# Squares, sums and transposed keys in the head stage of a hybrid layer: one change to a Trainium2 kernel

## The chip, the cores and the metric

The kernel runs on one core of a Trainium2 chip. The metric is the device time of one execution in microseconds (us), lower is better. Times of the kernel before are 1087.89 to 1088.5, median 1088.14 (3 runs); one more execution was profiled. The engines are called PE (TensorE, with its weight loads as PEld), DVE (VectorE), ACT (ScalarE), POOL (GpSimd) and SP (SyncE, which here only issues transfers). Each engine works through its own instructions in the order in which the program issues them; semaphores tie the engines together.

## What is computed

One layer over 256 positions of width 2048, all float32. Of the reference, this is what matters here:

```python
qa, ka, va, fa, qb, kb, vb = jnp.split(h @ w_in_l, splits, axis=-1)     # h = rms_norm(x)
qa = rms_norm(to_heads(qa, N_HEADS_FOX), q_norm_l)       # 8 heads of 128, normalized head by head
ka = rms_norm(to_heads(ka, N_HEADS_FOX), k_norm_l)
out_a = forgetting_attention(qa, ka, to_heads(va, N_HEADS_FOX), c)      # softmax(q k / sqrt(d) + c_t - c_s) v
out_b = stick_breaking_attention(to_heads(qb, N_HEADS_SB), to_heads(kb, N_HEADS_SB), to_heads(vb, N_HEADS_SB))
merged = jnp.concatenate([rms_norm(from_heads(out_a), out_norm_fox_l),
                          rms_norm(from_heads(out_b), out_norm_sb_l)], axis=-1)
x = x + merged @ w_out_l
x = x + conv_ffn(rms_norm(x), ...)                       # up, causal convolution, gate, down
```

The head norms of qa and ka need, for every position and head, the sum of 128 squares.

## The kernel before

**Products in two parts.** Each weight tile arrives as float32 in `w_raw` (5 buffers, loaded by SP, 1 MB each). ACT casts it to a rounded part `w_hi` (line 277, 3 buffers), DVE subtracts to get the rest `w_lo` (line 285, called "split" below). PE multiplies with both: eight matmuls with `w_hi`, four with `w_lo`, twelve for one product of four row blocks (`in_three`, line 305).

**Units and steps.** The combined projection is done in five units (`unit`, lines 546 to 632): A holds the queries and keys of the first four forgetting heads, B those of the second four, C the first stick-breaking queries and keys, V the stick-breaking values, D the second stick-breaking queries and keys. A unit is 11 steps that form a scheme of seven products with fewer multiplications and four plain ones. Steps 4, 6, 9 and 11 are plain and hold two sets of twelve matmuls, the others one. Weights of a step are loaded six steps ahead (sums of two weight tiles, line 593, four steps ahead, and accumulating transfers on POOL's queue), cast and split two steps ahead. The results of a product are taken out of a PSUM bank by ACT (line 601) or added by DVE (line 607), and a bank is written again by a later step, which waits for that. Among these, DVE's addition out of bank a behind step 7 is issued at step 8, after the cast and split for step 10, and step 9's second set writes bank a again.

**Turns.** Side work is written as Python generators. `tick` (line 246) advances them all by one `yield`; it is called after every step and in the middle of every plain step. This is a "turn": turns 1, 2, 3 belong to steps 1, 2, 3, turns 4 and 5 to step 4, 6 to step 5, 7 and 8 to step 6, 9 to step 7, 10 to step 8, 11 and 12 to step 9, 13 to step 10, 14 and 15 to step 11. The order of all instructions on each engine follows from it, with no reordering later. In a turn the running heads go first, then their products in plain float32 (what stands behind `yield FLOATS`, lined up for all heads that reach it in that turn), then the other tasks. Heads wait in a queue, and one starts at most every third turn (`STAGGER`).

**Rows to heads.** When a unit is finished, its `done` function is one of the other tasks of the next unit. For the forgetting heads it is `fox_rows(half)` (line 693): half 0 runs in the turns of unit B, half 1 in those of unit C. Before, turn by turn: turns 1 to 4 square one of four row tiles each (128 positions by 4 heads of 128; keys first, `order`), with four activations per tile whose accumulator gives the sum of squares of one head. At turn 4 DVE starts the reciprocal root (line 171), at turn 6 ACT takes logarithm and exponential, DVE ends it and multiplies the two key tiles (line 710), at turn 7 the two query tiles.

- Half 0 sends its keys `kA0` through the transposing transfer at turn 7 (`send_heads`): ACT spreads the float32 words into planes of 16 bits (line 646), SP issues two transposing transfers (line 650). The queries are transposed on PE at turn 9 (`to_heads`, line 687) and taken out by ACT at turn 10 (line 691), and behind that the keys' planes are joined again (`take_heads`, line 655, one tile on ACT, one on DVE). Heads 0 to 3 may start from turn 11 on.
- Half 1 transposes the keys `kA1` on PE at turn 8, takes them out at turn 9 and transposes the queries there, takes these out at turn 10. Heads 4 to 7 may start from turn 11 on.

A forgetting head (`fox_head`, line 787) splits its queries and keys (792 on ACT, 793 on DVE), two turns later multiplies them on PE (798 to 804) and has DVE mask and take the maxima (807 to 810), two turns later takes exponentials (816, 817) and DVE scales (819 to 821), and so on to its output at line 860, thirteen turns after its start.

**Stick-breaking heads.** `sb_rows(1)` sends the keys `kB1` through the transfer, transposes the queries on PE one turn later, takes them out at the next, and joins the keys (line 655, both tiles on ACT) at the turn behind that. In `sb_head`, after a head's output, DVE adds the head's squares to a running sum (line 923) behind the output's low part (line 919).

Of the kernel before, what the change touches and what calls it, by code (L numbers as in the profile page):

```python
# [12 lines left out]
AF = mybir.ActivationFunctionType  # L13
ALU = mybir.AluOpType
AX = mybir.AxisListType
# [4 lines left out]
NT = S // P  # L20
KT = D // P
HD = 128
NH = 8
# [24 lines left out]
def hybrid_layer(  # L48
# [20 lines left out]
    act, dve = nc.scalar, nc.vector  # L69
# [43 lines left out]
    gq = const.tile([P, 1], F32, name="gq")  # L113
# [20 lines left out]
    zeros = ccol.rearrange("p a b -> p (a b)")[:, :P]  # L134
# [204 lines left out]
    oFox = late.tile([P, NH, S], F32, name="oFox")  # L339
# [11 lines left out]
    def heads_tile(name):  # L351
        return at.tile([P, 4, S], F32, name=name, tag="qk", bufs=2)
# [25 lines left out]
    tile_of = {}  # L378
# [264 lines left out]
    def send_turned(rows, room, moves=(act.copy, dve.tensor_copy)):  # L643
        planes = room.bitcast(U16).rearrange("p h s -> p (h s)").rearrange("p (t c) -> p t c", t=NT)
        for t, (move, (source, words)) in enumerate(zip(moves, rows)):
            move(
                planes[:, t].rearrange("p (b f) -> p b f", b=2),
                source.bitcast(U16).rearrange("p (f b) -> p b f", b=2),
            )
            nc.sync.dma_start_transpose(  # L650
                words.bitcast(U16).rearrange("p (g s) -> p g s", s=P), planes[:, t]
            )
# [7 lines left out]
    def send_heads(rows, n, key, moves=(act.copy, dve.tensor_copy)):  # L660
        tile_of[key] = heads_tile(key)
        send_turned([(rows[n, t], rows[n, t]) for t in range(NT)], tile_of[key], moves)

    def take_heads(rows, n, key, moves):
        for t, move in enumerate(moves):
            take_turned(move, rows[n, t], t, tile_of[key])
# [13 lines left out]
    def to_heads(rows, which, keys, scales):  # L680
        for n, key, scale in zip(which, keys, scales):
            dst = tile_of[key] = heads_tile(key)
            pss = []
            for t in range(NT):
                ps = psb.tile([P, 4, P], F32, name="ps_h", tag="t")
                for h in range(4):
                    nc.tensor.transpose(ps[:, h, :], rows[n, t][:, h * HD : (h + 1) * HD], ident)
                pss.append(ps)
            yield
            for t in range(NT):  # L690
                act.activation(dst[:, :, t * P : (t + 1) * P], pss[t], AF.Identity, scale=scale)

    def fox_rows(half):
        def done(rows):
            order = [(1, 0), (1, 1), (0, 1), (0, 0)]
            ss = small.tile([P, 4, 4], F32, name="ss", tag="ss")
            rn = small.tile([P, 4, 4], F32, name="rn", tag="rn")
            for m, nt in enumerate(order):
                for h in range(4):
                    act.activation(  # L700
                        zeros, rows[nt][:, h * HD : (h + 1) * HD], AF.Square,
                        accum_out=ss[:, m, h : h + 1],
                    )
                if m < 3:
                    yield
            flat = "p a b -> p (a b)"
            yield from rsqrt(rn.rearrange(flat), ss.rearrange(flat), 1.0 / HD, 16)
            for m, nt in enumerate(order):
                r3 = rows[nt].rearrange("p (h d) -> p h d", h=4)
                dve.tensor_tensor(r3, r3, rn[:, m, :].unsqueeze(2).to_broadcast([P, 4, HD]), op=ALU.mult)  # L710
                if m % 2:
                    yield
                    if m == 1 and not half:
                        send_heads(rows, 1, "kA0", (act.copy, act.copy))
            while started["fox"] < 4 * half:
                yield
            if half:
                yield from to_heads(rows, (1, 0), ("kA1", "qA1"), (1.0, gq))
            else:
                yield  # L720
                yield from to_heads(rows, (0,), ("qA0",), (gq,))
                take_heads(rows, 1, "kA0", (act.copy, dve.tensor_copy))
            for h in range(4 * half, 4 * half + 4):
                waiting.append(fox_head(h, half))

        return done

    def sb_rows(half):
        def done(rows):
            if half:  # L730
                while started["sb"] < 4:
                    yield
                yield
                send_heads(rows, 1, "kB1", (act.copy, act.copy))
                yield
                yield from to_heads(rows, (0,), ("qB1",), (QSCALE,))
                yield
                take_heads(rows, 1, "kB1", (act.copy, act.copy))
            else:
                while started["fox"] < NH:  # L740
                    yield
                yield
                yield
                yield from turned_heads(rows)
            ready.add(f"qB{half}")
            if "vB" in ready:
                start_sb(half)

        return done

    def start_sb(half):
        for h in range(4 * half, 4 * half + 4):
            waiting.append(sb_head(h, half))
# [111 lines left out]
    def sb_head(h, half):  # L865
        q, k = tile_of[f"qB{half}"][:, h % 4, :], tile_of[f"kB{half}"][:, h % 4, :]
        (hi, lo), v1 = tile_of["vB01"], tile_of["vB"][half, 1]
        yield FLOATS
        ps = psb.tile([P, 512], F32, name="ps_z", tag="t")[:, : 3 * P].rearrange("p (a b) -> p a b", a=3)
        z0, z1 = ps[:, 0:2, :].rearrange("p a b -> p (a b)"), ps[:, 2, :]  # L870
        zz = ps.rearrange("p a b -> p (a b)")
        mm = nc.tensor.matmul
        mm(z0, k[:, :P], q, start=True, stop=False)
        mm(z1, k[:, P:], q[:, P:], start=False, stop=True)
        started["sb"] += 1
        diagonal = ps[:, 0::2, :]
        dve.tensor_tensor(diagonal, diagonal, maskB, op=ALU.add)
        yield
        e = tmp.tile([P, 3 * P], F32, name="e", tag="pr")
        act.activation(e, zz, AF.Abs)  # L880
        act.activation(e, e, AF.Exp, scale=-1.0)
        act.activation(e, e, AF.Ln, bias=1.0)
        dve.scalar_tensor_tensor(e, zz, 0.0, e, op0=ALU.max, op1=ALU.add)
        yield
        yield
        sps = tmp.tile([P, 2, 3 * P], F32R, name="sps", tag="sps")
        act.copy(sps[:, 0, :], e)
        dve.tensor_tensor(sps[:, 1, :], e, f32(sps[:, 0, :]), op=ALU.subtract)
        yield
        yield  # L890
        for i in range(2):
            mm(zz, ntri[:, :P], sps[:, i, :], start=False, stop=False, skip_group_check=True)
        for i in range(2):
            mm(ps[:, 1, :], ntri[:, P:], sps[:, i, 2 * P :], start=False, stop=i == 1, skip_group_check=True)
        yield
        w = tmp.tile([P, 3 * P], F32, name="w", tag="pT")
        act.activation(w, zz, AF.Exp)
        if h < NH - 1:
            ws = tmp.tile([P, 2, 3 * P], F32R, name="ws", tag="sps")
            act.copy(ws[:, 0, :S], w[:, :S])  # L900
            dve.tensor_tensor(ws[:, 1, :S], w[:, :S], f32(ws[:, 0, :S]), op=ALU.subtract)
        yield
        po = psb.tile([P, S], F32, name="ps_o", tag="t")
        hs = slice((h % 4) * HD, (h % 4 + 1) * HD)
        h0 = slice(h * HD, (h + 1) * HD)
        if h < NH - 1:
            yield from weighted(po, hi[:, h0], lo[:, h0], v1[:, hs], ws, w[:, S:])
        else:
            yield FLOATS
            mm(po, tile_of["vB"][half, 0][:, hs], w[:, :S], start=True, stop=False)  # L910
            mm(po[:, P:], v1[:, hs], w[:, S:], start=False, stop=True)
        yield
        open_outputs()
        if h >= 2:
            oSb.append(rows_tile(f"oSb{h}", 0 if h >= 4 else 1, F32R).rearrange("p (a s) -> p a s", a=2))
        o = oSb[h]
        act.activation(o[:, 0, :], po, AF.Identity, scale=g_sb[:, h : h + 1])
        sq = squared(po, 1, h)
        dve.scalar_tensor_tensor(
            o[:, 1, :], po, g_sb[:, h : h + 1], f32(o[:, 0, :]), op0=ALU.mult, op1=ALU.subtract  # L920
        )
        if sq is not None:
            dve.tensor_tensor(ssq[1], ssq[1], sq, op=ALU.add)

    unit(0, WF, row_tiles("rA", 0), fox_rows(0))
# [609 lines left out]
```

## Time and profile before

| | us |
|---|---|
| median of 3 runs | 1088.14 |
| profiled execution | 1089.65 |
| span of the profiled execution (first to last instruction) | 1087.9 |
| PE busy | 1082.6 |
| DVE busy | 929.5 |
| ACT busy | 776.1 |
| granted clock of TensorE | 1.0 |

A row of the timeline gives the start and the duration in us, the engine, the line, the operation, what is written and read, how many instructions are merged (x2), and in brackets the idle time of the engine before it with what ended it. Merged rows give the time from the first start to the last end. A duration includes a tail in which the next instruction already runs, so a sum over many instructions goes by their starts. In the list of transfers the last number is the median time from issue to landing.

### The profile page before, as it was taken

The page shows a single profiled execution, that of the slowest core. Times are in us where ns is not written, and L with a number is a line of the kernel's source. Part 1 is how long each engine was busy: PE and PEld are TensorE (multiplying, and loading weights), DVE is VectorE, ACT ScalarE, POOL GpSimd, SP SyncE. Part 2 cuts the span into 40 slices and gives each one's busy share as a digit, 9 for nine tenths or more (in the row PEclk, how much of TensorE's full clock was granted, in tenths as well). Part 3 has the DMA queues.
Part 4 walks back from the last instruction along what each step waited for, and adds up shares of the span by engine and source line. Part 5 has one row for each costly group of instructions (what it writes and reads, how often), then busy time and mean ns, then how long its engine had stood idle before and what let it go on. Part 6 is the DMA issues. An engine that isn't in the chain of part 4 may idle for free.

```text
span 1087.9 us, 14614 instructions
## 1 busy us (share of the span) xinstructions
PE 1082.6 (100%) x5635; PEld 932.2 (86%) x5635; DVE 929.5 (85%) x928; ACT 776.1 (71%) x981; POOL 59.0 (5%) x53
## 2 busy tenths in 40 slices
PE   9999999999999999999999999999999999999998
PEld 9988888888878888888888888888888888888887
DVE  5988899898997877779888988889888898879896
ACT  6767798887876857667766767667767766667663
POOL 0000000001000000000000000000000010000000
PEclk9999999999999999999999999999999999999999
DMA  8897988999876666579899597987969698996995
GB/s 311 267 274 234 306 190 241 245 258 290 244 231 222 193 201 195 192 182 263 252 242 300 172 274 250 255 287 178 310 195 294 219 245 261 232 308 168 284 244 156
DMA packets 192688, 262.85 MB, mean 242 GB/s; under 512 B 22105, under 2 KB 115691, under 8 KB 192619
## 3 DMA queue, kind: packets, MB, share of 16 engines
q1 hardware_dynamic: 169162, 214.59, 59.5%
q0 software_dynamic: 23280, 47.19, 24.5%
q8 instruction: 44, 0.72, 0.3%
q14 instruction: 26, 0.20, 0.1%
q10 hardware_dynamic: 176, 0.14, 0.0%
HBM read 255.48 MB, written 2.10 MB: 237 GB/s over the span
## 4 chain that ended last, share of the span: by engine, by line
PE 89%; DVE 5%; issue 2%; DMA 2%; ACT 1%; DVEq 0%; ACTq 0%; POOLq 0%
PE pu L1268 41%; PE bank_a L305 16%; PE bank_b L305 10%; PE bank_c L305 6%; PE acc_o L305 5%; PE acc_v L425 4%; PE bank_e L305 3%; DVE w_lo L285 2%; DMA w_raw<-in_w_down_dram 2%; PE acc L305 2%; ACT w_hi L277 1%; PE ps_x L195 1%; PE ps_o L775 0%; DVE w_raw L996 0%; DVE xb L1290 0%
## 5 line engine op out<-in xcount | busy, mean ns | idle before, releaser
L285 DVE TENSOR_TENSOR w_lo<-w_raw,w_hi 128x2048 fp32r<-128x2048 f32 (+2 forms) x251 | 555.7, 2218 | 120.5 <-ACT w_hi L277 119.6
L277 ACT CAST w_hi<-w_raw 128x2048 fp32r<-128x2048 f32 (+2 forms) x251 | 464.4, 1853 | 205.1 <-PE pu L1268 84.4
L1268 PE MATMUL pu<-hT,w_hi 128*128 128x512 f32 x1408 | 333.5, 389 | 0.0
L1268 PEld LDWEIGHTS pu<-hT,w_hi 128*128 128x128 f32 x1408 | 262.9, 188 | 53.7
L1268 PEld LDWEIGHTS pu<-hT,w_lo 128*128 128x128 f32 x1408 | 180.0, 191 | 6.6
L1268 PE MATMUL pu<-hT,w_lo 128*128 128x256 f32 x1408 | 182.0, 283 | 0.0
L1321 POOL DMA_DIRECT2D w_raw<-in_w_down_dram x31 | 39.8, 1302 | 714.7 <-DVE w_lo L285 383.1
L1193 ACT ACTIVATE tap<-up,ccol 128x256 f32<-128x256 f32 x176 | 74.6, 495 | 0.0
L305 PE MATMUL bank_a<-w_hi,hT 128*128 128x512 f32 x192 | 48.6, 395 | 0.0
L305 PEld LDWEIGHTS bank_a<-w_hi,hT 128*128 128x128 f32 x192 | 35.2, 188 | 6.9
L305 PE MATMUL bank_b<-w_hi,s 128*128 128x512 f32 x160 | 40.1, 392 | 0.2 <-DVE xb L1290 0.2
L305 PE MATMUL bank_a<-w_hi,s 128*128 128x512 f32 x160 | 40.0, 392 | 0.0
L305 PE MATMUL bank_a<-w_hi,g 128*128 128x512 f32 x152 | 38.0, 392 | 0.0
L425 PE MATMUL acc_v<-w_hi,hT 128*128 128x344 f32 x192 | 36.1, 330 | 0.0
L305 PEld LDWEIGHTS bank_b<-w_hi,s 128*128 128x128 f32 x160 | 28.8, 189 | 5.8 <-issue 0.6
L305 PEld LDWEIGHTS bank_a<-w_hi,s 128*128 128x128 f32 x160 | 28.9, 189 | 5.2
L1186 ACT ACTIVATE gate<-up,ccol 128x256 f32<-128x256 f32 x44 | 24.1, 594 | 11.5 <-DVE up L1179 6.2
L1198 DVE TENSOR_TENSOR gate<-gate,tap 128x512 f32<-128x512 f32 x44 | 30.3, 688 | 2.3
L1198 DVE TENSOR_TENSOR val<-val,tap 128x512 f32<-128x512 f32 x44 | 30.3, 688 | 2.3
L305 PE MATMUL acc_o<-w_hi,oSb 128*128 128x512 f32 x128 | 31.7, 396 | 0.0
L1179 DVE TENSOR_TENSOR up<-t,R 128x512 f32<-128x512 f32 x44 | 30.5, 692 | 1.5
L305 PEld LDWEIGHTS bank_a<-w_hi,g 128*128 128x128 f32 x152 | 27.4, 189 | 5.0
(312 smaller groups left out, 1427.4 us busy)
## 6 DMA issues: line engine op xcount, KB each, us to landing
w_raw<-in_w_up_dram SPq DMA_DIRECT2D x88, 1024.0 KB, 6.8
w_raw<-in_w_down_dram SPq DMA_DIRECT2D x44, 1024.0 KB, 7.1
w_raw<-in_w_in_dram SPq DMA_DIRECT2D x40, 1024.0 KB, 6.8
w_raw<-in_w_down_dram POOLq DMA_DIRECT2D x31, 1024.0 KB, 9.9
w_raw<-in_w_out_dram SPq DMA_DIRECT2D x16, 1024.0 KB, 6.2
w_raw<-in_w_in_dram POOLq DMA_DIRECT2D x10, 1024.0 KB, 9.9
w_raw<-in_w_in_dram SPq DMA_DIRECT2D x13, 516.0 KB, 5.3
xb<-in_x_dram POOLq DMA_DIRECT2D x4, 512.0 KB, 9.3
```

The costliest lines, as they stand in the source:

```text
L195: nc.tensor.transpose(ps[:, j, t * P : (t + 1) * P], x2[:, t, (k + j) * P : (k + j + 1) * P], ident)
L277: copy(hi[:, :n], raw[:, :n])
L285: dve.tensor_tensor(lo[:, :n], raw[:, :n], f32(hi[:, :n]), op=ALU.subtract)
L305: nc.tensor.matmul(o, lhs(i, l, t), r[:, i, :] if cut is None else r[:, i, cut], start=starts and j == 0, stop=stops and j == 3 * n - 1, s ...
L425: nc.tensor.matmul(banks[j][t][:, :VC], of_half(hT[:, k], l, t), w[:, 0, m * VC : (m + 1) * VC], start=k == l == 0 and w is mem["parts", i ...
L1179: dve.tensor_tensor(u[:, :, 2:], t2, R, op=ALU.mult)
L1186: act.activation(a[:, j, :], u[:, j, 2:], AF.Identity, scale=ccol[:, 2, f : f + 1], bias=ccol[:, 3, f : f + 1],)
L1193: act.activation(taps[w][:, j, :], u[:, j, w : w + S], AF.Copy, scale=ccol[:, w, f : f + 1])
L1198: dve.tensor_tensor(a, a, tap, op=ALU.add)
L1268: nc.tensor.matmul(acc[:, j, S:] if low else acc[:, j, :], (lo if low else hi)[:, i, j * P : (j + 1) * P], hT[:, k, 0, :] if low else hT[: ...
L1321: nc.gpsimd.dma_start(mem[weights].rearrange("p (a b) -> p a b", a=4), plus, accum_op=ALU.add)
```

## The change

The change has four parts, and one of them holds for both halves of the forgetting heads:

1. Both halves square whole row tiles: one activation of 128x512 per tile, written into `oFox` (the later outputs of the forgetting heads, not yet in use), two tiles per turn; one turn later DVE sums each into four numbers. The squares take turns 1 and 2 and the sums turns 2 and 3, so all that follows comes one turn earlier.
2. The second four heads' keys `kA1` go through the transposing transfer as the first four's do, with the second half of `oFox` as the room for the planes: sent at turn 6, joined at turn 7 by ACT. The queries are transposed on PE at turn 7, in the place where the keys were transposed before, and taken out at turn 8; heads 4 to 7 may start from turn 9 on.
3. The second stick-breaking keys `kB1` are joined one turn earlier, right behind the queries' eviction.
4. In the stick-breaking heads but the last, the addition of the squares is issued one turn later.

For half 0 the turns become: sums 2 and 3, key rows multiplied at 5, keys sent and query rows multiplied at 6, queries transposed at 8, taken out at 9 with the keys' joining behind, heads from 10 on.

```diff
-            for m, nt in enumerate(order):
-                for h in range(4):
-                    act.activation(
-                        zeros, rows[nt][:, h * HD : (h + 1) * HD], AF.Square,
-                        accum_out=ss[:, m, h : h + 1],
-                    )
-                if m < 3:
-                    yield
+            for first in (0, 2):
+                squared = [oFox[:, 2 * m : 2 * m + 2, :].rearrange("p a s -> p (a s)") for m in (first, first + 1)]
+                for m, rows_squared in enumerate(squared):
+                    act.activation(rows_squared, rows[order[first + m]], AF.Square)
+                yield
+                for m, rows_squared in enumerate(squared):
+                    dve.tensor_reduce(
+                        ss[:, first + m, :], rows_squared.rearrange("p (h d) -> p h d", h=4),
+                        axis=AX.X, op=ALU.add,
+                    )
...
                 if m % 2:
                     yield
-                    if m == 1 and not half:
-                        send_heads(rows, 1, "kA0", (act.copy, act.copy))
+                    if m == 1:
+                        if half:
+                            room = oFox[:, 4:8, :]
+                        else:
+                            room = tile_of["kA0"] = heads_tile("kA0")
+                        send_turned([(rows[1, t], rows[1, t]) for t in range(NT)], room, (act.copy, act.copy))
...
             if half:
-                yield from to_heads(rows, (1, 0), ("kA1", "qA1"), (1.0, gq))
+                tile_of["kA1"] = heads_tile("kA1")
+                take_heads(rows, 1, "kA1", (act.copy, act.copy))
+                yield from to_heads(rows, (0,), ("qA1",), (gq,))
...
                 yield from to_heads(rows, (0,), ("qB1",), (QSCALE,))
-                yield
                 take_heads(rows, 1, "kB1", (act.copy, act.copy))
+                yield
...
         if sq is not None:
+            if h < NH - 1:
+                yield
             dve.tensor_tensor(ssq[1], ssq[1], sq, op=ALU.add)
```

More of the change, by code (lines that the diff above doesn't have):

```diff
@@ L736, in done @@
                 yield from to_heads(rows, (0,), ("qB1",), (QSCALE,))
+                take_heads(rows, 1, "kB1", (act.copy, act.copy))
                 yield
-                take_heads(rows, 1, "kB1", (act.copy, act.copy))
             else:
```

## The prediction

> **What bounds the kernel now.** I read the page first, then the busy time in the stage that the change touches, then the engines' timelines there.
>
> ```profile
> span 1087.9 us, 14614 instructions
> ...
> PE 1082.6 (100%) x5635; PEld 932.2 (86%) x5635; DVE 929.5 (85%) x928; ACT 776.1 (71%) x981; POOL 59.0 (5%) x53
> ```
> ```profile
> 140.00:185.00 45.00, 45.00 (x226) 37.96 (x225) 42.22 (x61) 42.92 (x89) 1.62 (x2) 1.00 0.88 245
> ```
> TensorE (PE) practically never rests. So only two things move the end: work taken off PE, and new waits of PE. The second row (columns: length, PE, weight loads, DVE, ACT, POOL, clock, DMA share, GB/s) is unit C, where the second four forgetting heads are prepared: DVE has 2.8 us to spare in 45 and ACT 2.1. What arrives one turn too late there stops PE, and what stops PE here is not won back later.
>
> **The change on PE.** The second keys' eight transposes go.
>
> ```profile
> 158.09 1.98 PE L305 MATMUL bank_e<-w_hi,hT 128*128 128x512 f32 x8
> 159.90 1.07 PE L305 MATMUL bank_e<-w_lo,hT 128*128 128x512 f32 x4
> ...
> 162.05 2.09 PE L305 MATMUL bank_b<-w_hi,hT 128*128 128x512 f32 x8
> ...
> 164.89 1.04 PE L687 MATMUL ps_h<-cs,rB 128*128 128x128 f32 x8
> 165.68 2.11 PE L305 MATMUL bank_a<-w_hi,sums 128*128 128x512 f32 x8
> 167.63 1.10 PE L305 MATMUL bank_a<-w_lo,sums 128*128 128x512 f32 x4
> ```
> Eight transposes run from 164.89 to 165.68 (0.79), and the eight products behind them take 1.95 to the next set (165.68 to 167.63) instead of 1.81 (158.09 to 159.90): 0.93 us saved. I take 0.14 for the switch behind every group of plain float products. Counting turns: both halves reach the heads earlier, the first by one turn, the second by two, so the heads of the two halves no longer stand a multiple of three turns apart and stop sharing a turn for their float products. I count 15 groups instead of 14 in units B to V, one of them saved with the keys, so two are new: 0.28 lost.
>
> Three small waits of PE should shrink.
>
> ```profile
> 107.76 0.30 PEld L305 LDWEIGHTS bank_b<-w_hi,hT 128*128 128x128 f32 x2 [0.35 <-ACT rB L601]
> ...
> 301.31 0.30 PEld L874 LDWEIGHTS ps_z<-qB,kB 128*128 128x128 f32 x2 [0.30 <-ACT kB L655]
> ...
> 304.54 0.19 PEld L305 LDWEIGHTS acc_o<-w_hi,hT 128*128 128x128 f32 x1 [0.41 <-DVE xb L1104]
> ```
> ```profile
> 303.08 0.41 DVE L923 TENSOR_TENSOR ssq<-ssq,osq 128x256 f32<-128x256 f32 x1
> ```
> At 107.76 PE waits for an eviction that stands behind squares on ACT: 0.2 of it goes. At 301.31 it waits for the joined stick-breaking keys, which now go ahead of a weight cast that nobody needs before 304.54; but 3 us later PE waits for DVE anyway, so that 0.30 is kept only as far as DVE comes earlier. It does by 0.33, since the addition of 303.08 (0.41, but 0.33 to the next start) no longer stands ahead of the accumulator's reading. I take 0.35 for both. The other moved additions change order only and cost nothing while DVE has the turn's 3 us. Sum of the gains: 0.93 - 0.28 + 0.20 + 0.35 = 1.2 us.
>
> **The change on ACT and DVE.** Per half, sixteen squares become four, and DVE gets four sums.
>
> ```profile
> L700 ACT ACTIVATE ccol<-rB x16: 302/312/324, 140.9 to 155.0; 128x128 f32<-128x128 f32 x16
> ```
> ```profile
> 156.52 0.29 DVE L809 TENSOR_REDUCE nm<-ps_s 128x1 f32<-128x128 f32 x1
> 156.72 0.41 DVE L810 TENSOR_REDUCE nm<-ps_s 128x1 f32<-128x256 f32 x1
> ...
> 157.13 0.42 DVE L852 TENSOR_TENSOR pT<-ps_p,pT 128x256 fp32r<-128x256 f32 x1
> ...
> 161.13 0.16 DVE L819 RECIPROCAL rl<-l 128x2 f32<-128x2 f32 x1
> ...
> 161.79 0.17 DVE L176 TENSOR_TENSOR rs_u<-rs_a,rs_y 128x16 f32<-128x16 f32 x1
> ...
> 162.62 1.29 DVE L710 TENSOR_TENSOR rB<-rB,rn 128x512 f32<-128x512 f32 x2
> 163.83 2.28 DVE L285 TENSOR_TENSOR w_lo<-w_raw,w_hi 128x2048 fp32r<-128x2048 f32 x1
> 166.03 0.42 DVE L807 TENSOR_TENSOR ps_s<-ps_s,masksR 128x256 f32<-128x256 f32 x1
> ...
> 167.03 1.28 DVE L710 TENSOR_TENSOR rB<-rB,rn 128x512 f32<-128x512 f32 x2
> 168.23 0.42 DVE L852 TENSOR_TENSOR pT<-turned,pT 128x256 fp32r<-128x256 f32 x1
> ```
> Sixteen at 0.31 are 5.0 us of ACT, the accumulator readings behind them not counted; four wide ones of about 0.6 are 2.4. What ACT gains I count as nothing, because DVE or a transfer is what it waits for next. A sum of 128x512 isn't in the trace: 128 elements take 0.29 and 256 take 0.41, so 512 take about 0.65, and 0.60 from start to start as the multiplications of that width (1.21 for two). Bounds 0.35 and 0.70. Four are 2.4 us on DVE.
>
> *First wait, turn 7 of unit C.* Before, the query rows are normalized at turn 7 and transposed at turn 9: DVE's last multiplication is done at 168.3, just as PE comes out of the four products that start at 167.63. After, they are normalized at turn 6 and transposed at turn 7, in the middle of step 6. PE is there at 162.05 on this trace's clock (the head's products that now stand ahead stand at turn 6, so the sum of PE's work up to there is the same). DVE's program up to there, from the split for step 4, which starts at 147.13 before:
>
> ```profile
> 128.15 2.29 DVE L285 TENSOR_TENSOR w_lo<-w_raw,w_hi 128x2048 fp32r<-128x2048 f32 x1 [1.07 <-ACT w_hi L277]
> ...
> 132.02 2.29 DVE L285 TENSOR_TENSOR w_lo<-w_raw,w_hi 128x2048 fp32r<-128x2048 f32 x1 [0.39 <-ACT w_hi L277]
> ...
> 147.13 2.28 DVE L285 TENSOR_TENSOR w_lo<-w_raw,w_hi 128x2048 fp32r<-128x2048 f32 x1
> ```
> One more pair of L793 stands ahead of it, and head operations that come a turn earlier can fill the two waits of 1.07 and 0.39: I take 147.2, give or take 0.7. Then four splits at 2.20 (163.83 to 166.03), four sums at 0.60, the norms' first step 0.1, two sets of reciprocal and scaling at 0.66, two of mask and maximum at 1.00, the subtractions of L852 and L793 0.95, the rest of the norms 0.83 (161.79 to 162.62), four multiplications at 0.60: 8.8 + 2.4 + 0.1 + 1.3 + 2.0 + 0.95 + 0.83 + 2.4 = 18.8, so 166.0. PE waits 166.0 - 162.05 = 3.9 us. Bounds: sums at 0.35 and the start 0.7 earlier, 2.2; the other ends, 5.0.
>
> *Second wait, unit B, step 9.* The norms now stand ahead of the split for step 7 on DVE, and a load on SP's queue waits for that split, with the keys' transposes behind it.
>
> ```profile
> 115.26 0.37 SPq L271 DMA_DIRECT2D w_raw<-in_w_in_dram  x1
> 117.77 1.61 SPq L650 DMA_TRANSPOSE rA<-kA  x1
> ```
> ```profile
> 124.98 1.36 ACT L655 COPY kA<-rA 128x1024 uint16<-128x1024 uint16 x1 [0.97 <-DMA rA<-kA]
> ```
> ```profile
> 103.13 4.72 DVE L285 TENSOR_TENSOR w_lo<-w_raw,w_hi 128x2048 fp32r<-128x2048 f32 x2
> ...
> 125.66 0.74 DVE L607 SCALAR_TENSOR_TENSOR rB<-bank_a,nrstd,rB 128x512 f32<-128x512 f32 x1
> ```
> ```profile
> 128.06 1.98 PE L305 MATMUL bank_a<-w_hi,hT 128*128 128x512 f32 x8
> ```
> From 103.13: four splits 8.8, sums 2.4, norms 0.9, two multiplications 1.2, together 13.3, so the split for step 7 ends at 116.5 (115.23 before), the load goes out, and the first transpose at 117.0. Before it was usable 7.2 us after its issue (117.77 to 124.95): 124.2. ACT's joining copy now stands ahead of the cast for step 10 (before, that cast went first). Copy 1.3, cast 1.8, split 2.2, the addition out of bank a 0.7: 130.2. PE wants to write bank a again at 128.0. A wait of 2.2 us, between 0 (landing 5 us after issue) and 3.5.
>
> *Third wait, unit C, step 9.* The same for the second keys, with more in the way.
>
> ```profile
> 116.70 2.00 ACT L646 COPY kA<-rA 128x1024 uint16<-128x1024 uint16 x2 [0.59 <-DVE rA L710]
> ...
> 159.96 0.68 ACT L601 ACTIVATE rC<-bank_a,nrstd 128x512 f32<-128x512 f32 x1
> ...
> 165.10 1.91 ACT L277 CAST w_hi<-w_raw 128x2048 fp32r<-128x2048 f32 x1
> ...
> 298.67 2.58 ACT L655 COPY kB<-rD 128x1024 uint16<-128x1024 uint16 x2
> ```
> ```profile
> rA<-kA SPq DMA_TRANSPOSE x2, 5.4
> rD<-kB SPq DMA_TRANSPOSE x2, 7.2
> ```
> DVE ends the split for step 7 at 163.7 (166.0 less 2.2), the load behind it goes, the first transpose at 164.2, usable at 171.4 with 7.2 (kB1's figure, also right behind a load) or 169.6 with 5.4. ACT has its first key row at 161.0 (166.0 less 1.2, 1.0, 2.2 and 0.6), spreads the planes in 2.0, has the work from the eviction at 159.96 to the cast at 165.10 to do (5.1), reaches the joining copies at about 168.2 and stands still; behind them are queued the fourth head's exponentials, the queries' eviction (together 2.0) and the cast for step 9 (1.8). Copies 2.6: the cast is done at 177.8 or 176.0. PE, 3.9 late, wants it at 176.0. Then the split, the addition out of bank a and the fifth head's subtraction follow late too, and PE waits again at the second half of step 9, by some 2.2. Together 4.6 or 2.5; I take 3.5, bounds 1.0 and 5.5.
>
> Sum: 2.2 + 3.9 + 3.5 - 1.2 = 8.4 us. Against the profiled execution's 1089.65 that is 1098.05; its time is 1.5 above the median of the runs, 1088.14, from which the forecast is 1096.5.
>
> [...] In unit C's row DVE has 2.8 us left and the sums need 2.4, so by saturation alone nothing would wait (1086.9, rival 1); by the order of the turns it is 1096.5.
>
> **Rivals.**
> 1. *Nothing waits* (chance 0.15): DVE and the landings come in time, and only the gain is left, 1088.14 - 1.2 = 1086.9, no change. It holds if DVE has its query rows by 162.05, 3.9 us sooner than my count. For it: ACT is relieved, and its casts held DVE up before. Against it: DVE's rows from 161.13 to 168.23 stand end to start.
> 2. *Only the first wait* (0.15): the transposes land early, as 3 to 4 us would do. 1088.14 + 3.9 - 1.2 = 1090.8.
> 3. *The load queue is late too* (0.09): the DMA share is 0.88 in unit C, two more transposes delay weights as well, and landings of 10 us add some 4 us: 1100.5.
> 4. *The clock falls* (0.06): a wait of 3.9 us is the longest in the kernel.
>
> ```profile
> L189 PE MATMUL ps_i<-ccol x12: 421/421/579, 1.1 to 4.4; 128*128 128x128 f32 x12
> ```
> At the start, after idling, this shape takes 421 ns from 1.1 to 4.4, while eight transposes of that shape take 1.04 us together above: less than half the pace for some 3.5 us. If the wait brings that back, 3.5 us of work take 1.8 more: 1098.3. [...]
>
> That the keys still cross PE is excluded: the second half's call names the queries alone.
>
> **How the numbers follow.** The forecast itself has 0.55, its own range 1093.5 to 1099.5. About 0.2% (2.2 us) is what a measurement of this kernel tells from no change: bounds 1085.96 and 1090.32. Slower: 0.55 + 0.09 + 0.06 + 0.09 of rival 2 = 0.79. Same: 0.06 of rival 2 and 0.10 of rival 1. Faster: 0.05, the part of rival 1 in which more of PE's small waits go. The range 1088.0 to 1100.5 leaves out most of rival 1 and half of rival 3.
>
> **What would show it.** In the changed profile PE should wait at the queries' transposes of the second half for DVE's multiplication of the query rows, 3 to 4 us; at step 9 of units B and C for the addition out of bank a; ACT should stand before both joining copies for a DMA. Transposes of rB should be 8 instead of 16. If PE's waits in units B and C stay under 1 us together, the ladder for DVE is wrong, and the time is near 1087.

## The result and the profile after

The changed kernel takes 1097.3 us (median of 5 runs, 1097.03 to 1098.01) against 1088.17 (5 runs beside it): ratio 1.0083, 95% interval 1.0071 to 1.0094. It is slower by about 9 us. Its profiled execution took 1098.01, with a span of 1096.2 (before: 1089.65 and 1087.9).

The page of the changed kernel: its span, busy times and granted clock in 40 slices.

```profile
span 1096.2 us, 14557 instructions
...
PE 1085.2 (99%) x5627; PEld 933.4 (85%) x5627; DVE 934.1 (85%) x936; ACT 771.6 (70%) x927; POOL 59.3 (5%) x53
...
PEclk9999998999999999999999999999999999999999
```

PE is busy 2.6 us more, although it has eight transposes less, and one slice shows a lower clock. That slice is unit C. The timeline of PE there, changed kernel:

```profile
162.34 1.07 PE L305 MATMUL bank_e<-w_lo,hT 128*128 128x512 f32 x4
166.89 1.94 PE L687 MATMUL ps_h<-cs,rB 128*128 128x128 f32 x8 [3.48 <-ACT ssq L789]
168.48 3.76 PE L305 MATMUL bank_b<-w_hi,hT 128*128 128x512 f32 x8
172.04 1.48 PE L305 MATMUL bank_b<-w_lo,hT 128*128 128x512 f32 x4
173.36 2.03 PE L305 MATMUL bank_a<-w_hi,sums 128*128 128x512 f32 x8
```

From the last matmul's start at 163.02 to 166.89 there are 3.87 us instead of 0.23: a wait of 3.65 at the queries' transposes. Then these take 1.59 to the next set instead of 0.79, and the twelve matmuls from 168.48 to 173.36 take 4.88 instead of 2.86 (167.84 to 170.70 in the run with the wait filled, below): another 2.8 us at half pace. The windows of the changed kernel (length; PE, weight loads, DVE, ACT, POOL; clock, DMA share, GB/s) and DVE's timeline tell why:

```profile
163.00:167.00 4.00, 0.52 (x3) 0.14 (x2) 3.97 (x7) 4.00 (x6) 0.00 (x0) 0.88 1.18 333
167.00:173.00 6.00, 6.00 (x19) 5.04 (x20) 3.00 (x5) 5.97 (x11) 0.00 (x0) 0.51 0.98 249
```
```profile
162.26 2.28 DVE L285 TENSOR_TENSOR w_lo<-w_raw,w_hi 128x2048 fp32r<-128x2048 f32 x1
164.47 0.42 DVE L815 TENSOR_TENSOR ps_s<-ps_s,masksR 128x256 f32<-128x256 f32 x1
...
165.46 1.28 DVE L712 TENSOR_TENSOR rB<-rB,rn 128x512 f32<-128x512 f32 x2
```

The releaser that the wait's row names (ACT, line 789) isn't the real one: what the transposes read, the query rows, DVE finishes at 166.74, just before PE goes on. And the granted clock is 0.51 behind the pause. The other waits are smaller. Changed kernel, list of PE's waits (total, times, longest):

```profile
PE bank_b L305 <- ACT vB L601: 1.1, 1, 1.1
...
PE bank_a L305 <- DVE rB L607: 0.4, 1, 0.4
```

By PE's starts, the longer first matmul behind a wait included, the first is 1.36 us at 208.81 in unit V, the second 0.68 at 128.53 in unit B. The one in unit V is new: the eviction (line 601) stands on ACT behind a head's joining copy, and that waits for its transposing transfer:

```profile
205.43 1.06 ACT L846 COPY turned<-pr 128x768 uint16<-128x768 uint16 x1 [1.35 <-DMA pr<-turned]
...
208.08 0.68 ACT L601 ACTIVATE vB<-bank_b,rstd 128x512 f32<-128x512 f32 x1
```

The sum by starts: 3.65 + 2.8 + 1.36 + 0.68, some 1.5 in small waits of DVE and ACT (at 158.69, 253.03, 312.47, 331.86 and 353.26), less 0.93 of transposes and 0.2 at 107.76: 8.9, against 8.3 of the spans; the rest isn't placed.

### The profile page after: what moved, and what is told of

It reads as the page before. It is cut to its first block, busy times and chain, and to the rows that moved or that the text cites. A ratio compares the mean times of both kernels' runs of the same rounds, so it can differ in the third digit from the quotient of the medians.

```text
span 1096.2 us, 14557 instructions
## 1 busy us (share of the span) xinstructions
PE 1085.2 (99%) x5627; PEld 933.4 (85%) x5627; DVE 934.1 (85%) x936; ACT 771.6 (70%) x927; POOL 59.3 (5%) x53
## 4 chain that ended last, share of the span: by engine, by line
PE 85%; DVE 7%; ACT 3%; issue 3%; DMA 2%; DVEq 0%; ACTq 0%
PE pu L1278 45%; PE bank_a L305 14%; PE bank_b L305 8%; PE acc_v L425 4%; PE acc_o L305 4%; PE bank_c L305 4%; DVE w_lo L285 3%; PE acc L305 2%; ACT w_hi L277 2%; PE bank_e L305 1%; DMA pr<-turned 1%; DMA w_raw<-in_w_out_dram 1%; PE ps_x L195 1%; DMA rA<-kA 0%; DVE ss L704 0%
```

## The experiments

Three theories at first. *Place*: the loss comes from where the query transposes stand, one turn behind their multiplication. *DVE's load*: eight sums are too much for it wherever PE asks. *Transfer*: the two more transposing transfers and their copies do it. Later a fourth, *ACT's load*, took the place of the first. Ratios are against the kernel before, run on the same chip, with 95% intervals.

**Keys back on PE** (all but part 2).

```diff
-    if m == 1:
-        if half:
-            room = oFox[:, 4:8, :]
-        else:
-            room = tile_of["kA0"] = heads_tile("kA0")
-        send_turned([(rows[1, t], rows[1, t]) for t in range(NT)], room, (act.copy, act.copy))
+    if m == 1 and not half:
+        send_heads(rows, 1, "kA0", (act.copy, act.copy))
...
 if half:
-    tile_of["kA1"] = heads_tile("kA1")
-    take_heads(rows, 1, "kA1", (act.copy, act.copy))
-    yield from to_heads(rows, (0,), ("qA1",), (gq,))
+    yield from to_heads(rows, (1, 0), ("kA1", "qA1"), (1.0, gq))
```

> The changed kernel (1097.3) with part 2 undone: the second half's keys cross PE again, at turn 7, and its queries at turn 8, so the query transposes stand two turns behind their multiplication. Place theory (the loss comes from where the query transposes stand): PE reaches them at about 163.0 + 0.9 + 2.9 = 166.8, DVE's multiplication ends at 166.7, so the wait of 3.65 goes and with it the half clock (2.8); eight transposes come back (0.93): about 1090.5 (1090.0 to 1091.6, the lower end if unit V's wait of 1.3 goes too). Load theory (DVE has too much to do with the eight sums, wherever PE asks): the late rows show at other places, over 1094. Transfer theory (the two more transposing transfers and their joining copies do it): all of the loss goes, about 1088.

Measured 1090.13 us, ratio 1.0018 (1.0009 to 1.0027). Its timeline of PE:

```profile
162.23 1.08 PE L305 MATMUL bank_e<-w_lo,hT 128*128 128x512 f32 x4
163.15 1.04 PE L687 MATMUL ps_h<-cs,rB 128*128 128x128 f32 x8
163.94 2.07 PE L305 MATMUL bank_b<-w_hi,hT 128*128 128x512 f32 x8
165.85 1.07 PE L305 MATMUL bank_b<-w_lo,hT 128*128 128x512 f32 x4
166.78 1.06 PE L687 MATMUL ps_h<-cs,rB 128*128 128x128 f32 x8
```

There is no wait here and no fall of the clock (1.00 from 160 to 185 us), and unit V's wait is gone too; the one in unit B stays (0.55). With the sums still on DVE, its load alone is out as the main cause. Place and transfer both remain: part 2 is where the loss sits.

**Queries one turn later**, transfers as they are.

```diff
     take_heads(rows, 1, "kA1", (act.copy, act.copy))
+    yield
     yield from to_heads(rows, (0,), ("qA1",), (gq,))
```

> The changed kernel with one more turn between the joining of kA1 and the queries' transposes; all transfers and sums stay. Place theory: PE reaches the transposes after the twelve matmuls of the next set, at about 163.0 + 2.9 = 165.9, and waits some 0.85 for the multiplication that ends at 166.7; the clock stays full: 1097.3 - 2.8 - 2.8 = 1091.7, or 1090.4 if unit V's wait goes as the heads start one turn later. Load theory: DVE's work is the same and shows elsewhere, 1095 or more. Transfer theory: the transfers are the same, 1097.

Measured 1096.16, ratio 1.0075 (1.0062 to 1.0088): place misses by 4.5 us. The first wait did shrink to 0.9 at full clock (1.00 from 163 to 173 us), as that theory says, but at step 9 PE now stops for the addition out of bank a and goes on at half pace. PE of this run, and ACT ahead of it:

```profile
166.28 1.06 PE L687 MATMUL ps_h<-cs,rB 128*128 128x128 f32 x8 [0.75 <-ACT ssq L790]
...
179.35 2.93 PE L305 MATMUL bank_a<-w_hi,hT 128*128 128x512 f32 x6 [2.42 <-DVE rC L607]
```
```profile
161.16 2.00 ACT L646 COPY oFox<-rB 128x1024 uint16<-128x1024 uint16 x2 [2.90 <-DVE rB L712]
...
168.22 2.56 ACT L655 COPY kA<-rB 128x1024 uint16<-128x1024 uint16 x2
...
171.45 1.90 ACT L277 CAST w_hi<-w_raw 128x2048 fp32r<-128x2048 f32 x1
```

ACT stands 2.9 us in front of the spreading copies, because DVE's key rows come late, and from then on it works without a break, with 4.5 us of copies in the row; the joining copies find their data there. The casts come late, DVE's splits wait for them, and the addition out of bank a stands behind a split.

**The wait filled** with matmuls on zeros, so that PE isn't idle; first 34, then 16 of them.

```diff
     take_heads(rows, 1, "kA1", (act.copy, act.copy))
+    idle(16)
     yield from to_heads(rows, (0,), ("qA1",), (gq,))
```

> The changed kernel with 34 matmuls of 128x128 on zeros (109 ns each by the first pass of such rows at full pace, 3.7 us) on PE ahead of the queries' transposes of the second half: PE waits as long for DVE, but is not idle. If the pause is what lowers the granted clock, the clock stays at 1.0 behind it and the 2.8 us of slow work go: 1094.5 (1094.3 to 1095.0). If the slow work has another cause (transfers, DVE, power of the whole chip), it stays: 1097.3 to 1097.6.

Measured 1098.39, ratio 1.0092 (1.0078 to 1.0106), a miss by the experiment's own size: 34 of them are 68 passes.

```profile
163.61 7.75 PE L189 MATMUL ps_i<-ccol 128*128 128x128 f32 x68
171.20 1.04 PE L687 MATMUL ps_h<-cs,rB 128*128 128x128 f32 x8
```

> The changed kernel with 16 zero matmuls of 128x128 on PE ahead of the queries' transposes of the second half. The run with 34 showed that each is two passes (68 rows, 163.61 to 171.20), so that PE came 4.3 us later than without them; 16 are 32 passes, 3.5 us, and end before DVE's multiplication does (166.7). Pause theory (the granted clock falls because PE stands still for 3.5 us): the transposes start as in the changed kernel, the clock stays at 1.0, and 2.8 us of slow work go: 1094.5. But the late start of step 9 was also a cover for ACT: if with PE back on time the addition out of bank a is late at step 9, as it was by 2.4 in the run one turn later, part of that comes back: up to 1096. If the clock falls for another reason: 1097.3.

Measured 1096.97, ratio 1.0080 (1.0066 to 1.0093). PE in the run with 16:

```profile
163.36 3.73 PE L189 MATMUL ps_i<-ccol 128*128 128x128 f32 x32
167.02 1.06 PE L687 MATMUL ps_h<-cs,rB 128*128 128x128 f32 x8
167.84 2.10 PE L305 MATMUL bank_b<-w_hi,hT 128*128 128x512 f32 x8
...
181.68 2.14 PE L305 MATMUL bank_a<-w_hi,hT 128*128 128x512 f32 x8 [1.18 <-DVE rC L607]
```

In both runs the clock stays at 1.0 behind the filling: here the pause is what lowered it. But of the 2.8 us of slow work the median wins 0.3 and the profiled span 1.2, since PE now waits at step 9. DVE's addition out of bank a in the changed kernel and in this run:

```profile
180.73 0.74 DVE L607 SCALAR_TENSOR_TENSOR rC<-bank_a,nrstd,rC 128x512 f32<-128x512 f32 x1
```
```profile
180.88 0.74 DVE L607 SCALAR_TENSOR_TENSOR rC<-bank_a,nrstd,rC 128x512 f32<-128x512 f32 x1
```

It stands at the same time with and without PE's slow clock. So ACT and DVE set how early step 9 can go on, whatever PE's pace. Of the 6.45 us of first wait and slow clock, PE would have had to spend all but 1.2 there: it starts the set behind this addition at 181.68 with the wait filled and at 182.92 in the changed kernel.

**Part 2 alone**, on the kernel before, in the place that the change gives it: half 1's keys sent as in the change, the queries alone transposed, one turn behind their multiplication.

```diff
-    if m == 1 and not half:
-        send_heads(rows, 1, "kA0", (act.copy, act.copy))
+    if m == 1:
+        if half:
+            room = oFox[:, 4:8, :]
+        else:
+            room = tile_of["kA0"] = heads_tile("kA0")
+        send_turned([(rows[1, t], rows[1, t]) for t in range(NT)], room, (act.copy, act.copy))
...
-    yield from to_heads(rows, (1, 0), ("kA1", "qA1"), (1.0, gq))
+    tile_of["kA1"] = heads_tile("kA1")
+    take_heads(rows, 1, "kA1", (act.copy, act.copy))
+    yield from to_heads(rows, (0,), ("qA1",), (gq,))
```

> The kernel before (1088.2) with part 2 alone: squares and sums on ACT as before, the second half's keys by the transposing transfer, queries transposed at turn 8, one turn behind their multiplication. Place theory: PE is at the transposes at about 164.7, DVE's multiplication ends at 168.3, so PE waits 3.65 without any sum on DVE, and the clock falls: 1088.2 - 0.9 + 3.65 + 2.8 = 1093.7, or 1095 with the wait in unit V. Load theory: DVE has no more to do than before, 1088 or less. Transfer theory: the two transfers and their copies cost what the changed kernel lost, 1095 to 1097, with PE waiting for a joined key or a weight.

Measured 1094.84, ratio 1.0060 (1.0047 to 1.0074): a wait of 3.6 at the transposes and the half clock (0.72 on average from 167 to 173 us), with no sum on DVE. Place and transfer both allow this time; DVE's load doesn't. Its profiled execution (1093.91) speaks for place: the wait and 3.4 us at half clock (1.7 lost), less 0.93 of transposes, are 4.4 us, against 4.2 between the spans (1092.1 and 1087.9), and no other wait of PE behind the start is over 0.4.

**Parts 3 and 4 alone** (the edits at `kB1` and `ssq[1]`, on the kernel before).

> The kernel before (1088.2) with parts 3 and 4 alone: the second stick-breaking keys joined one turn earlier, the squares' sums one turn later. By the prediction's step they gain 0.35: 1087.85. By the changed kernel's trace, where the starts of PE around the accumulator's reading are 649 and 567 ns apart instead of 380 and 658, and 580 instead of 227 at a later head's product, they lose about 0.5: 1088.7. A joined copy placed elsewhere than where it can wait should not do more than that either way.

Measured 1089.14, ratio 1.0005 (0.9996 to 1.0014): no difference that these runs can tell; a gain of 0.35 would still lie in the interval. The trace shows why there is little to win. By PE's starts, the wait for the stick-breaking keys cost PE 0.16 in the kernel before, for the 0.30 of that row is idle time of the weight loads; here it is gone. Around the accumulator's reading PE loses 0.84 instead of 0.70, which takes it back.

**Keys joined behind the queries' eviction.** In the changed kernel, and with part 2 alone on the kernel before:

```diff
     tile_of["kA1"] = heads_tile("kA1")
-    take_heads(rows, 1, "kA1", (act.copy, act.copy))
+    yield
     yield from to_heads(rows, (0,), ("qA1",), (gq,))
+    take_heads(rows, 1, "kA1", (act.copy, act.copy))
```

> The changed kernel with the second half's keys handled as the first half's are: queries transposed at turn 8, taken out at turn 9, keys joined behind that. All sums and transfers stay; against the run one turn later (1096.2) only the place of the joining copies on ACT differs, which now stand behind the cast for step 9. Theory of the joining copies' place (2.4 us of copies ahead of the casts for steps 9 and 10 make the addition out of bank a late, which then lowers the clock): the waits of 2.4 and 0.3 at step 9 and the slow work behind them (1.5) go, the first wait of 0.8 stays: 1091.5 to 1092.5. Theory of ACT's load (the copies are too much for ACT in unit C, wherever they stand): the wait moves to step 10 or 11, 1094.5 to 1096.5.

> The kernel before (1088.2) with part 2 alone and late: keys sent at turn 7, queries transposed at turn 9 as before, taken out at turn 10, keys joined behind that; squares and sums on ACT as before. Place theory: PE loses its eight transposes (0.9) and no wait comes in: 1087.3. Load theory for ACT: spreading and joining add 4.5 us, the keys' eviction takes 1.15 away, and ACT has 2.1 us of idle time in unit C, so some 1.2 us come back as waits, and more with the clock: 1088.5 to 1091.

Measured: 1097.94, ratio 1.0086 (1.0073 to 1.0100), above what either theory gave; and 1091.59, ratio 1.0030 (1.0018 to 1.0041), above the range. The first of them, DVE and ACT, then PE:

```profile
173.09 2.57 ACT L655 COPY kA<-rB 128x1024 uint16<-128x1024 uint16 x2
175.51 1.92 ACT L277 CAST w_hi<-w_raw 128x2048 fp32r<-128x2048 f32 x1
```
```profile
177.47 2.29 DVE L285 TENSOR_TENSOR w_lo<-w_raw,w_hi 128x2048 fp32r<-128x2048 f32 x1 [2.43 <-ACT w_hi L277]
179.68 0.74 DVE L607 SCALAR_TENSOR_TENSOR rC<-bank_a,nrstd,rC 128x512 f32<-128x512 f32 x1
```
```profile
180.47 2.11 PE L305 MATMUL bank_a<-w_hi,hT 128*128 128x512 f32 x8 [3.12 <-DVE rC L607]
```

The copies now stand ahead of the next cast, and the split of that cast is the one that the addition stands behind. Moving the copies to this place on ACT doesn't help: the addition starts at 179.68, and at 178.55 in the run with the queries one turn later.

**Copies on POOL.** With part 2 alone and late: both kinds (and the heads one turn later), then the joining ones alone; and the joining ones alone in the changed kernel with its keys joined behind. The edit of the joining copies:

```diff
-    take_heads(rows, 1, "kA1", (act.copy, act.copy))
+    take_heads(rows, 1, "kA1", (nc.gpsimd.tensor_copy, nc.gpsimd.tensor_copy))
```

> The kernel before with part 2 as in the run with part 2 alone and late (1091.6), but the second keys' spreading and joining copies on POOL, which has 5% of its time busy, instead of ACT, and the heads one turn later. Theory of ACT's load (PE's waits of 1.0, 0.8, 0.7 and 0.6 in that run come from 4.5 us of copies less 1.15 of eviction on ACT): they go, and of the eight transposes 0.9 is won: 1087.4, or 1088.0 if POOL's joined keys come late for the fifth head. Transfer theory (the two more transposes on the load queue delay the weights): the waits stay, 1091 to 1092.

Measured 1094.11, ratio 1.0046 (1.0032 to 1.0060). The forecast of ACT's load is missed by over 6 us. Three of the four waits are gone; the fourth, at the transposes, grew from 0.8 to 2.7, as DVE's multiplication runs beside POOL's copies (one of them from 168.09 to 169.52), and one of 1.1 came in at 244.4 in unit D. DVE and PE:

```profile
167.65 2.36 DVE L710 TENSOR_TENSOR rB<-rB,rn 128x512 f32<-128x512 f32 x2
```
```profile
170.16 1.06 PE L687 MATMUL ps_h<-cs,rB 128*128 128x128 f32 x8 [2.52 <-DVE rB L710]
```

That step 9's wait is gone says nothing of ACT: PE came to it 1.9 us later, while DVE's addition out of bank a came no sooner (176.18, and 175.57 with the copies on ACT).

> The run with part 2 alone and late (1091.6) with only the joining copies of the second keys on POOL; the spreading ones stay on ACT, so that DVE's multiplication of the query rows is over before POOL's copies start (with both on POOL, that multiplication took 2.36 instead of 1.28 and PE waited 2.7 for it). Theory of ACT's load: 2.5 us leave ACT, spreading less eviction leaves it with 0.85 more than before, which its idle time takes: no wait over 0.3 at steps 7 to 10, and 0.9 is won on PE: 1087.7 (1087.4 to 1088.3). Rival (the load is as much DVE's, which POOL's copies slow down): a split of 3.1 instead of 2.2 makes PE wait again, 1089 to 1090. Rival (transfers): 1091.5.

Measured 1090.93, ratio 1.0021 (1.0012 to 1.0030): 0.7 us below the 1091.59 with the copies on ACT, with intervals that overlap, and 3.2 above what ACT's load forecast. The two waits in unit V are gone, but PE keeps 0.8 at the transposes, and at step 9 it waits 1.5 instead of 1.0. The addition out of bank a with the joining copies on ACT, then on POOL:

```profile
175.57 0.74 DVE L607 SCALAR_TENSOR_TENSOR rC<-bank_a,nrstd,rC 128x512 f32<-128x512 f32 x1
```
```profile
176.04 0.74 DVE L607 SCALAR_TENSOR_TENSOR rC<-bank_a,nrstd,rC 128x512 f32<-128x512 f32 x1
```

It comes 0.47 later; a split and a scaling ahead of it take 0.55 longer beside POOL's copies (2.60 instead of 2.29, 0.53 instead of 0.29). So with part 2 alone the joining copies on ACT aren't shown to be what step 9 waits for.

> The run with the changed kernel's second keys joined behind (1097.9) with only those joining copies on POOL. Theory of ACT's load: PE's waits for the additions out of bank a (3.3 at step 9 of unit C, 1.9 at step 9 of unit V) go or shrink to a few tenths, the waits of 0.7 in unit B and 0.9 at the queries' transposes stay: 1093 (1092 to 1094). Rivals as for the other run: 1095 if POOL slows DVE by a microsecond, 1097.9 if the transfers do it.

Measured 1094.38, ratio 1.0052 (1.0038 to 1.0066), just above the range of ACT's load and 3.6 us less than with the copies on ACT. Its PE at step 9:

```profile
178.25 2.12 PE L305 MATMUL bank_a<-w_hi,hT 128*128 128x512 f32 x8 [0.83 <-DVE rC L607]
```

The wait there fell from 3.3 to 1.0 with nothing changed but who copies, and the addition starts at 177.45 instead of 179.68. The transfers are the same in both, so they aren't the cause of that wait: in the changed kernel the joining copies on ACT are. The wait of 1.9 in unit V stayed, against what was expected.

**The first keys joined later**, in the run with the keys on PE.

```diff
     yield from to_heads(rows, (0,), ("qA0",), (gq,))
+    yield
     take_heads(rows, 1, "kA0", (act.copy, dve.tensor_copy))
```

> The run with the keys on PE (1090.1, parts 1, 3 and 4) with the first four heads' keys joined one turn later, at turn 10 and so behind the cast for step 10 instead of ahead of it. Theory of the joining copy's place (PE's wait of 0.55 at 127.6 for the addition out of bank a in unit B comes from the copy of 1.3 us that stands ahead of that cast on ACT): the wait goes, 1089.5. Rival (DVE's sums make the addition late): the wait stays, 1090.1. What is left above the kernel before is then the price of parts 3 and 4 (0.5) and of DVE's sums.

Measured 1091.48, ratio 1.0026 (1.0016 to 1.0036). PE in unit B goes through step 9 without a wait:

```profile
126.94 1.07 PE L305 MATMUL bank_c<-w_lo,hT 128*128 128x512 f32 x4
127.85 1.98 PE L305 MATMUL bank_a<-w_hi,hT 128*128 128x512 f32 x8
```

So that wait did come from the copy ahead of the cast. But the median rose by 1.3, with intervals that overlap: waits of 1.0, 0.5 and 0.4 appear in unit V and behind it. That they come because the first four heads now start a turn later against the second four wasn't tested.

No version beat the kernel before; nearest came the one with parts 3 and 4 alone, which can't be told from it.

## Why the prediction was right, and where not

The time was 0.8 us above the forecast and inside the range. The sum came out by luck, though: its errors cancel.

- **First wait**: forecast 3.9, measured 3.65, by the ladder that was counted: sums at 0.6 each, the query rows ready at 166.74, the pause where it was said. The third wait was reckoned with PE already this late.
- **The clock** (rival 4, chance 0.06): it came true, and cost 2.8, not 1.8, for the half pace lasted 6.8 us. The chance was mis-sized. Around an unfilled wait of about 3.6 at these transposes the clock fell in both kernels that had one (0.51 on average from 167 to 173 us in the changed kernel, 0.72 with part 2 alone), and with the wait filled it stayed at 1.0. The forecast's own pause was 3.9, so by these runs the two belonged together.
- **Second wait**: forecast 2.2, measured 0.68. The step that failed is that the keys' transposes stand behind a load that waits for the split for step 7. In the changed kernel they are issued one turn earlier and stand ahead of that load, which is the first of the three behind them:

```profile
105.57 7.38 SPq L271 DMA_DIRECT2D w_raw<-in_w_in_dram  x2
115.11 5.17 SPq L650 DMA_TRANSPOSE rA<-kA  x2
120.38 2.97 SPq L271 DMA_DIRECT2D w_raw<-in_w_in_dram  x3
```

  The transposes went out at 115.11, not 117.0, and the joining copy started at 122.36, not 124.2. The mechanism, the copy ahead of the cast, was right: ACT stood 0.95 us before that copy for the transfer, and the run with the first keys joined later takes the wait away.
- **Third wait**: forecast 3.5 with PE 3.9 late and at full pace, measured 0. The run with 16 filling matmuls is the case that was reckoned, and PE waits 1.2 there. The step that failed is ACT's standing still before the joining copies for a DMA. The transposes stand ahead of the load here too (162.85, the load at 165.63), the transfer landed in 3.3 us instead of 5.4 to 7.2, and ACT stood 2.9 us before the spreading copies, for DVE. Changed kernel, list of transfers (last number: median us to landing) and ACT's timeline:

```profile
rB<-oFox SPq DMA_TRANSPOSE x2, 3.3
```
```profile
161.78 2.00 ACT L646 COPY oFox<-rB 128x1024 uint16<-128x1024 uint16 x2 [2.89 <-DVE rB L712]
...
168.83 2.53 ACT L655 COPY kA<-rB 128x1024 uint16<-128x1024 uint16 x2
```

  So the cast for step 9 was done at 175.08, not at 176.0 to 177.8. In the changed kernel the half clock, which the sum left out, held PE back by another 2.8 us, and the addition was done at 181.47, before PE came. The lateness was real: where PE waited only 0.9 at the transposes (queries one turn later), it waited 2.6 there. What is taken off the first wait can come back in this one.
- **Gains**: the eight transposes are gone, and the 0.2 at 107.76 came. The 0.35 of parts 3 and 4 didn't: 0.16 is won at the stick-breaking keys, and around the accumulator's reading PE loses 0.87 instead of 0.70. The 0.28 for two more groups of float products is isolated by no run.
- **Not seen**: unit V's wait of 1.36. Its mechanism, the eviction behind a head's copy that waits for its transfer, is read from the trace; no run changed that alone.
- **DVE's load**: the prediction weighed it by unit C's idle time, 2.8 us for sums of 2.4. The runs show why idle time in a row is no measure: ACT's 2.9 us of standing still before the spreading copies are in that stretch too, and it has none left behind them.

What remains open: part 1 wasn't run by itself; the run with the keys on PE less that of parts 3 and 4, each against the kernel before beside it, puts it near 1.3 us. How much of step 9's lateness is ACT's and how much DVE's isn't settled either: with the joining copies on POOL, which slowed DVE, 1.0 to 1.5 us of it remain. Two medians (part 2 alone in its place, and both copies on POOL) lie 1 to 2 us above their profiled executions, so what their traces show is not all of it. With both copies on POOL the granted clock, told below, goes with that difference; with part 2 alone the profiled execution and the median one both show 0.998.

## What to carry to other kernels

When one engine is always busy, work taken off it is worth its time only if the engines that feed it have room at that place: 0.93 us of PE was bought here with 3.3 us of ACT (4.5 of copies less 1.2 of an eviction) in the stretch in which ACT had none. Two waits that hang on the same ladder of feeding work aren't independent, for what is taken off the first can come back in the second, so find that ladder's last step first. And a copy that waits stands in front of every cast behind it: look at what is queued behind it, not at how long it takes.

## What the hardware showed unexpectedly

**The length of a pause alone didn't decide whether the clock fell.** In the run with the queries one turn later, PE stood still for 2.4 us (and for 0.4 some two microseconds earlier) and the clock was halved; in the changed kernel with its keys joined behind, it stood still for 3.1 and the clock stayed in the profiled execution. Windows of the first, then of the second (clock is the third number from the end):

```profile
177.00:179.00 2.00, 0.00 (x0) 0.00 (x0) 2.00 (x2) 1.97 (x4) 0.00 (x0) 1.00 0.95 305
179.00:181.00 2.00, 1.65 (x4) 1.37 (x5) 1.50 (x5) 2.00 (x4) 0.00 (x0) 0.58 0.93 294
181.00:183.00 2.00, 2.00 (x6) 1.58 (x6) 1.60 (x1) 0.36 (x1) 0.00 (x0) 0.57 0.62 141
```
```profile
177.00:179.00 2.00, 0.36 (x2) 0.00 (x0) 1.53 (x1) 2.00 (x4) 0.00 (x0) 1.00 0.97 373
179.00:181.00 2.00, 0.53 (x2) 0.48 (x3) 2.00 (x4) 1.97 (x6) 0.00 (x0) 1.00 0.02 7
181.00:183.00 2.00, 2.00 (x10) 1.63 (x10) 1.09 (x4) 1.88 (x2) 0.00 (x0) 1.00 0.60 110
```

By what the windows lack of full clock, the half clock lasted 3.4 us in the first of them ((0.42 + 0.43) x 2 / 0.5) and 6.8 in the changed kernel ((0.12 x 4 + 0.49 x 6) / 0.5), once and twice the same length. So 2.4 us of pause were enough for a fall in one run, and 3.1 didn't bring it in the other; what decided between them is not shown by any run here.

Executions of one kernel differ in the same way. With both copies on POOL, where the profiled pause was 2.5 us, the mean granted clock was 1.0 in the two executions of 1092.2 and 1092.4 us and 0.998 in the three of 1094.1 to 1094.6. By an estimate from the 3.4 us above, one such stretch at half clock lowers the mean of an execution of 1092 us by 0.0016 and costs up to 1.7 us, so it fits; only one of the five was traced.

**POOL's copies slowed DVE.** Beside them (both copies on POOL) a multiplication pair of 1.28 us took 2.36 and a split of 2.29 took 3.12. Two joining copies took 4.66 us on POOL (joining ones alone) against 2.56 on ACT. So moving these copies to POOL wasn't free for DVE; why DVE took longer beside them, no run shows.
